# Attention's two score products per head: one wait for both banks, and the two issued side by side

## The chip, the cores and the metric

The kernel runs on one core of a Trainium2 chip. The metric is the device time of one execution in microseconds (us); lower is better. Of the kernel before there are three timed runs and one profiled execution.

## What is computed

The reference is a two-layer trunk over 512 tokens of width 1024. Each layer adds half a SwiGLU block, then a token mixer of four branches, then another half SwiGLU block:

```
for l in range(DEPTH):
    h = h + 0.5 * swiglu_ffn(rmsnorm(h, ...), ...)
    h = h + hybrid_token_mixer(rmsnorm(h, ...), l, ...)
    h = h + 0.5 * swiglu_ffn(rmsnorm(h, ...), ...)
return rmsnorm(h, final_norm)
```

The change is in the first branch, differential attention, with 4 heads. Each head has two sets of queries and keys (c = 0 and 1) of 64 channels each, and one set of values of 128 channels. A query sees the keys of its own chunk of 64 tokens and of all earlier ones:

```
s = jnp.einsum('bqhcd,bkhcd->bhcqk', q_blk, k)
p = jax.nn.softmax(jnp.where(allowed, s, -jnp.inf), axis=-1)
a = p[:, :, 0] - lam * p[:, :, 1]
return jnp.einsum('bhqk,bkhd->bqhd', a, v)
```

So each head and each block of 128 queries needs two score products that contract over only 64 channels. Everything is float32.

## The kernel before

The weights are streamed from HBM in tiles of 128x1024. Each tile is split into a rounded part `whi` (a CAST on ScalarE, L151) and a remainder `wlo` (a subtraction on VectorE), and every dense product runs as three one-pass products on TensorE. In the mixer's feature products these are the lines L157, L158 and L159. Eight k-steps of them, 24 products of 512 columns, make one output tile.

In each layer's mixer three things are issued in one stretch. The RWKV branch (`rwkv`) is one stream; attention (`diff_attn`), then GLA, then SSD are the other; and a `filler` of gate projections (`gate`: 24 products of L157 to L159, then a sigmoid on ScalarE into the tile `sg`, then a store by the SyncE queue) is put between their steps by `cotrace`, from costs written into the code. That fixes the order in which the code is traced. The order that each engine finally executes is then fixed when the program is built: a scheduler takes instructions by priority and by when it believes them ready. Each engine works through its own list in order and waits on semaphores. `chained(last, fn)` makes `fn`'s instruction stand behind `last` in that list; `prio(d)` shifts the priority.

Attention runs over 4 query blocks (qb 0 to 3) and in each over 4 heads (h 0 to 3). For a block the keys number n = 128, 256, 384 or 512. One head does this:

- two score products (L972), into two PSUM banks `sc[0]` and `sc[1]` of the tag `oy`, which has exactly two. The product of c = 0 reads partitions 0 to 63 of the queries and keys, that of c = 1 partitions 64 to 127. Since the operands are plain float32, each product is two instructions on TensorE. There are 16 heads and blocks a layer, so 64 products and 128 instructions in all;
- per bank a small memset for the mask (L974), a row maximum on VectorE (L976, `mx`), and an exponential with row sum on ScalarE (a helper, L100, tile `dap`), which shows as an ACTIVATE and an ACTIVATION_READ_ACCUMULATOR;
- on VectorE the scaling and the difference of the two, then transposes on TensorE (L987), a copy back on ScalarE (L989) and the products with the values (L993, `dv`).

The next head's products write the same two banks, so the product of c = 0 waits until the exponential of c = 0 of the head before has read its bank, and likewise for c = 1. Nothing ties the two products to each other.

Two more lines are named below. L761 is the last row of a triangular inversion that RWKV does row by row on VectorE in the same stretch; its result goes through two rounds of DMA to the products of L790. L647 and L634 are small TensorE steps of RWKV.

Of the kernel before, what the change touches and what calls it, by code (L numbers as in the profile page):

```python
# [13 lines left out]
AF = mybir.ActivationFunctionType  # L14
# [59 lines left out]
class Body:  # L74
# [815 lines left out]
    def diff_attn(self, ydst):  # L890
        nc = self.nc
        mm = nc.tensor.matmul
        dp = self.cp
        lam_init = 0.8 - 0.6 * math.exp(-0.3 * self.l)
        lam = self.g2((128, 256), name="lam")
        nc.sync.dma_start(out=lam, in_=self.a["lam"][self.l].partition_broadcast(128))
        lt = self.g2((128, 2, 64), name="lt")
        for j in range(2):
            self.mul(lt[:, j, :], lam[:, 128 * j : 128 * j + 64], lam[:, 128 * j + 64 : 128 * j + 128])
        ls = dp.tile([128, 2], F32, name="ls")  # L900
        nc.vector.tensor_reduce(out=ls, in_=lt, axis=AX.X, op=ALU.add)
        self.act(ls, ls, AF.Exp)
        nlam = dp.tile([128, 1], F32, name="nlam")
        self.sub(nlam, ls[:, 1:2], ls[:, 0:1])
        self.ts(nlam, nlam, -lam_init, ALU.add)
        gda = dp.tile([128, 1], F32, name="gda")
        self.ts(gda, self.p("da_n"), 1.0 - lam_init, ALU.mult)
        cos = self.c("cos").rearrange("p (t f) -> p t f", t=NT)
        sin = self.c("sin").rearrange("p (t f) -> p t f", t=NT)
        qT = []  # L910
        yield 0, 0

        def rope(ps, t, sc, sink):
            b = self.g2((128, 8, 2, 32), name="ropeb")
            o = self.g2((128, 16, 32), name="ropeo")
            c16 = cos[:, t : t + 1, :].to_broadcast([128, 16, 32])
            s8 = sin[:, t : t + 1, :].to_broadcast([128, 8, 32])
            p4 = ps.rearrange("p (h s f) -> p h s f", h=8, s=2)
            self.stt(o, ps.rearrange("p (h f) -> p h f", h=16), sc, c16, ALU.mult, ALU.mult)
            self.stt(b[:, :, 0, :], p4[:, :, 1, :], -sc, s8, ALU.mult, ALU.mult)  # L920
            self.stt(b[:, :, 1, :], p4[:, :, 0, :], sc, s8, ALU.mult, ALU.mult)
            of = o.rearrange("p h f -> p (h f)")
            self.add(of, of, b.rearrange("p h s f -> p (h s f)"))
            pt = self.small("os", (128, 4, 128))
            for h in range(4):
                nc.tensor.transpose(pt[:, h, :], of[:, h * 128 : (h + 1) * 128], self.ident)
            if isinstance(sink, list):
                for h in range(4):
                    nc.scalar.copy(sink[h][:, t * 128 : (t + 1) * 128], pt[:, h, :])
            else:  # L930
                nc.scalar.copy(sink, pt)

        def freed(pst):

            for t in range(2):
                o = self.g2(name="tk")
                nc.scalar.copy(o, pst[t])
                pst[t] = o
            return pst

        xs = (lambda k: self.xh[:, k, :], lambda k: self.xl[:, k, :])
        pk = self.tok(self.wt("dk"), *xs)
        kT = [self.g2(name="kT") for _ in range(4)]
        yield 20.8, 0.378
        pk = freed(pk)
        for t in range(NT):
            rope(pk[t], t, 1.0, kT)
            yield 0.4, 0.735
        pq = self.tok(self.wt("dq"), *xs)
        yield 20.8, 0.16  # L950
        pq = freed(pq)
        for t in range(NT):
            q = self.g2((128, 4, 128), name="qT")
            rope(pq[t], t, 0.125, q)
            qT.append(q)
            yield 0.4, 3
        pv = self.tok(self.wt("dv"), *xs)
        v = []
        for t in range(NT):
            vt = self.g2(name="dv")  # L960
            nc.scalar.copy(vt, pv[t])
            v.append(vt)
        yield 20.8, 0.702
        for qb in range(NT):
            n = (qb + 1) * 128
            o = self.g2((128, 4, 128), name="dao")
            for h in range(4):
                pr, l2 = [], dp.tile([128, 2], F32, tag="l2", bufs=2, name="l2")
                sc = [self.small("oy") for _ in range(2)]
                for c in range(2):  # L970
                    cp_ = slice(64 * c, 64 * c + 64)
                    mm(out=sc[c][:, 0:n], lhsT=qT[qb][cp_, h, :], rhs=kT[h][cp_, 0:n], start=True, stop=True)  # L972
                for c, s in enumerate(sc):
                    nc.vector.memset(s[0:64, n - 64 : n], -3.0e38)  # L974
                    mx = dp.tile([128, 1], F32, tag="mx", bufs=4, name="mx")
                    nc.vector.tensor_reduce(out=mx, in_=s[:, 0:n], axis=AX.X, op=ALU.max, negate=True)  # L976
                    e = self.g2(name="dap")
                    self.act(e[:, 0:n], s[:, 0:n], AF.Exp, bias=mx[:, 0:1], accum_out=l2[:, c : c + 1])
                    pr.append(e)
                r2 = dp.tile([128, 2], F32, tag="r2", bufs=2, name="r2")  # L980
                nc.vector.reciprocal(r2, l2)
                self.mul(r2[:, 1:2], r2[:, 1:2], nlam)
                self.ts(pr[0][:, 0:n], pr[0][:, 0:n], r2[:, 0:1], ALU.mult)
                self.stt(pr[0][:, 0:n], pr[1][:, 0:n], r2[:, 1:2], pr[0][:, 0:n], ALU.mult, ALU.add)
                pt = self.small("os", (128, 4, 128))
                for kb in range(qb + 1):
                    nc.tensor.transpose(pt[:, kb, :], pr[0][:, kb * 128 : (kb + 1) * 128], self.ident)  # L987
                at = pr[1].rearrange("p (k q) -> p k q", k=4)
                nc.scalar.copy(at[:, 0 : qb + 1, :], pt[:, 0 : qb + 1, :])  # L989
                po = self.small("os", (128, 128))  # L990
                last = None
                for kb in range(qb + 1):
                    last = self.chained(last, lambda: mm(  # L993
                        out=po, lhsT=at[:, kb, :], rhs=v[kb][:, h * 128 : (h + 1) * 128], start=kb == 0, stop=kb == qb))
                nc.vector.tensor_copy(o[:, h, :], po)
                yield 0.6 + 0.4 * qb, 2 + 0.7 * qb
            sq = self.g2((128, 4, 128), name="dasq")
            self.act(sq, o, AF.Square)
            ss = dp.tile([128, 4], F32, tag="das", bufs=2, name="das")
            nc.vector.tensor_reduce(out=ss, in_=sq, axis=AX.X, op=ALU.add)  # L1000
            self.ts(ss, ss, 1.0 / 128, ALU.mult, EPS, ALU.add)
            rs = dp.tile([128, 4], F32, tag="dar", bufs=2, name="dar")
            self.rsqrt(rs, ss, dp, "da")
            self.mul(o, o, rs.unsqueeze(2).to_broadcast([128, 4, 128]))
            pt = self.small("os", (128, 4, 128))
            for h in range(4):
                nc.tensor.transpose(pt[:, h, :], o[:, h, :], self.ident)
            self.act(o, pt, AF.Identity, scale=gda[:, 0:1])
            nc.sync.dma_start(out=ydst[:, :, qb * 128 : (qb + 1) * 128], in_=o)
            yield 0.4, 1.65  # L1010
# [465 lines left out]
```

## Time and profile before

| | |
|---|---|
| timed runs | 3089.2, 3090.36 and 3090.7 us; median 3090.36 |
| the profiled execution's own time | 3089.28 us, of which the profile's span is 3087.5 us |
| granted TensorE clock over the span | 0.998 of full speed |
| busy share of the span | TensorE 99%, VectorE 51%, ScalarE 37%, GpSimd 4% |
| stretches with attention's score products | 497 to 655 us (layer 0), 2031 to 2189 us (layer 1) |

An engine's share is an average over the whole program. What a change in one stage is worth is read in that stage: from the times at which instructions start there, and from what each waits for.

### The profile page before, as it was taken

What the parts mean: (1) busy time and instruction counts of PE and PEld (TensorE: products, weight loads), DVE (VectorE), ACT (ScalarE), POOL (GpSimd) and SP (SyncE); (2) the same over time, 40 slices, a digit from 0 to 9 for tenths busy, and PEclk for the clock granted to TensorE, in tenths of its full rate; (3) what the DMA queues carried; (4) which work ended last, traced back from release to release, by engine and by line L of the source; (5) the groups of instructions that cost most, each with busy time, mean ns of one, the idle gap of its engine ahead of it and who ended that gap; (6) DMA issues with size and microseconds to landing.
All of it is one profiled execution on the core that took longest, in us unless ns stands there. A gap on an engine that the chain in (4) does not pass through costs nothing. (4 is left out here: it accounts for less than half of the span.)

```text
span 3087.5 us, 40904 instructions
## 1 busy us (share of the span) xinstructions
PE 3044.8 (99%) x16212; PEld 2421.4 (78%) x16212; DVE 1587.4 (51%) x3229; ACT 1151.8 (37%) x1806; POOL 112.0 (4%) x148
## 2 busy tenths in 40 slices
PE   9999999999999999999999999999999999999999
PEld 7888887767777788888888888876777767888887
DVE  4332355857386875332343324558664968643323
ACT  4222345655332324222232223456544333232222
POOL 0000000001011100000000000000000111000000
PEclk9999999999999999999999999999999999999999
DMA  4222332322222554222342223223232325532222
GB/s 165 97 100 96 110 121 77 109 77 96 97 91 76 180 172 150 96 99 99 106 140 96 97 100 129 92 91 106 72 100 92 96 70 197 174 137 98 100 96 82
DMA packets 138450, 337.98 MB, mean 109 GB/s; under 512 B 35089, under 2 KB 43665, under 8 KB 137490
## 3 DMA queue, kind: packets, MB, share of 16 engines
q1 hardware_dynamic: 138112, 335.10, 32.7%
q8 instruction: 127, 2.08, 0.3%
q14 instruction: 65, 0.53, 0.1%
q10 hardware_dynamic: 146, 0.27, 0.0%
HBM read 297.03 MB, written 38.27 MB: 109 GB/s over the span
## 5 line engine op out<-in xcount | busy, mean ns | idle before, releaser
L81 DVE TENSOR_TENSOR wlo<-wraw,whi 128x1024 fp32r<-128x1024 f32 x478 | 585.3, 1225 | 873.2 <-ACT whi L151 859.7
L151 ACT CAST whi<-wraw 128x1024 fp32r<-128x1024 f32 x478 | 502.2, 1051 | 1397.6 <-PE pb L158 558.2
L157 PE MATMUL pb<-xh,whi 128*128 128x512 f32 x2064 | 821.2, 398 | 0.8 <-ACT s L100 0.8
L158 PE MATMUL pb<-xl,whi 128*128 128x512 f32 x2064 | 813.4, 394 | 0.0
L159 PE MATMUL pb<-xh,wlo 128*128 128x512 f32 x2064 | 809.8, 392 | 0.0
L157 PEld LDWEIGHTS pb<-xh,whi 128*128 128x128 f32 x2064 | 387.6, 188 | 98.5 <-issue 14.8
L158 PEld LDWEIGHTS pb<-xl,whi 128*128 128x128 f32 x2064 | 387.7, 188 | 81.9 <-issue 5.2
L159 PEld LDWEIGHTS pb<-xh,wlo 128*128 128x128 f32 x2064 | 387.8, 188 | 79.6 <-issue 1.0
L81 DVE TENSOR_TENSOR s<-s,pb 128x512 f32<-128x512 f32 x88 | 60.5, 687 | 303.0 <-PE pb L159 284.2
L100 ACT ACT_TABLE_LOAD x113 | 145.0, 1283 | 7.6 <-PE os L1252 3.9
L157 PE MATMUL pb<-yh,whi 128*128 128x512 f32 (+2 forms) x272 | 105.6, 390 | 0.0
L158 PE MATMUL pb<-yl,whi 128*128 128x512 f32 (+2 forms) x272 | 103.8, 382 | 0.7 <-DVE yl L81 0.7
L159 PE MATMUL pb<-yh,wlo 128*128 128x512 f32 (+2 forms) x272 | 103.6, 381 | 0.0
L157 PE MATMUL oy<-xh,whi 128*128 128x512 f32 x192 | 77.3, 403 | 5.8 <-DVE conv L97 5.5
L207 PE MATMUL pb<-whi,xh 128*128 128x512 f32 x192 | 76.6, 399 | 0.0
L158 PE MATMUL oy<-xl,whi 128*128 128x512 f32 x192 | 76.5, 398 | 0.0
L159 PE MATMUL oy<-xh,wlo 128*128 128x512 f32 x192 | 76.4, 398 | 0.0
L208 PE MATMUL oy<-wlo,xh 128*128 128x512 f32 x192 | 76.2, 397 | 0.0
L209 PE MATMUL pb<-whi,xl 128*128 128x512 f32 x192 | 76.1, 398 | 0.0
L207 PE MATMUL oy<-whi,xh 128*128 128x512 f32 x192 | 75.5, 393 | 0.0
L209 PE MATMUL oy<-whi,xl 128*128 128x512 f32 x192 | 75.5, 393 | 0.0
L208 PE MATMUL pb<-wlo,xh 128*128 128x512 f32 x192 | 75.5, 393 | 0.0
(421 smaller groups left out, 4570.8 us busy)
## 6 DMA issues: line engine op xcount, KB each, us to landing
wraw<-in_ffn_gu SPq DMA_DIRECT2D x176, 512.0 KB, 3.2
wraw<-in_win_f SPq DMA_DIRECT2D x118, 512.0 KB, 3.3
wraw<-in_ffn_d SPq DMA_DIRECT2D x88, 512.0 KB, 3.2
wraw<-in_win_t SPq DMA_DIRECT2D x48, 512.0 KB, 3.3
gd<-sg SPq DMA_DIRECT2D x64, 256.0 KB, 2.2
wraw<-in_wbr SPq DMA_DIRECT2D x32, 512.0 KB, 3.6
msg<-gd SPq DMA_DIRECT2D x64, 256.0 KB, 3.1
wraw<-in_wout SPq DMA_DIRECT2D x16, 512.0 KB, 3.2
```

The lines of the kernel that those rows point to most:

```text
L81: return (eng or self.nc.vector).tensor_tensor(out=out, in0=in0, in1=in1, op=op)
L100: return self.nc.scalar.activation(out=out, in_=in_, func=func, **kw)
L151: self.chained(behind[0], lambda: nc.scalar.copy(hi, raw))
L157: mm(out=ps, lhsT=lh, rhs=rh, start=first, stop=False)
L158: mm(out=ps, lhsT=lh, rhs=rl, start=False, stop=False)
L159: return mm(out=ps, lhsT=ll, rhs=rh, start=False, stop=last)
L207: mm(out=pst[t], lhsT=lh(k)[:, lt], rhs=hi[:, c], start=k == 0, stop=False)
L208: mm(out=pst[t], lhsT=lh(k)[:, lt], rhs=low[:, c], start=False, stop=False)
L209: mm(out=pst[t], lhsT=ll(k)[:, lt], rhs=hi[:, c], start=False, stop=k == nk - 1)
```

## The change

Three things are added, all in the loop over heads:

- ahead of a head's score products ScalarE copies one element into the first of the two banks. This copy is chained behind `ex`, the last exponential of the head before. As it writes the bank into which the product of c = 0 will go, that product has to wait for it;
- the product of c = 1 is chained behind that of c = 0, and its priority is moved up by 2000;
- the exponentials are chained to each other, through all heads and blocks.

```
+        ex = None
         for qb in range(NT):
             n = (qb + 1) * 128
             o = self.g2((128, 4, 128), name="dao")
             for h in range(4):
                 pr, l2 = [], dp.tile([128, 2], F32, tag="l2", bufs=2, name="l2")
                 sc = [self.small("oy") for _ in range(2)]
+
+                self.chained(ex, lambda: nc.scalar.copy(sc[0][0:1, 0:1], self.ident[0:1, 0:1]))
+                last = None
                 for c in range(2):
                     cp_ = slice(64 * c, 64 * c + 64)
-                    mm(out=sc[c][:, 0:n], lhsT=qT[qb][cp_, h, :], rhs=kT[h][cp_, 0:n], start=True, stop=True)
+                    with self.prio(-2000 * c):
+                        last = self.chained(last, lambda: mm(
+                            out=sc[c][:, 0:n], lhsT=qT[qb][cp_, h, :], rhs=kT[h][cp_, 0:n], start=True, stop=True))
                 for c, s in enumerate(sc):
                     nc.vector.memset(s[0:64, n - 64 : n], -3.0e38)
                     mx = dp.tile([128, 1], F32, tag="mx", bufs=4, name="mx")
                     nc.vector.tensor_reduce(out=mx, in_=s[:, 0:n], axis=AX.X, op=ALU.max, negate=True)
                     e = self.g2(name="dap")
-                    self.act(e[:, 0:n], s[:, 0:n], AF.Exp, bias=mx[:, 0:1], accum_out=l2[:, c : c + 1])
+                    ex = self.chained(ex, lambda: self.act(
+                        e[:, 0:n], s[:, 0:n], AF.Exp, bias=mx[:, 0:1], accum_out=l2[:, c : c + 1]))
                     pr.append(e)
```

Below the edit the line numbers of the changed kernel are 7 higher than before in most places: its score products are L977, its one-element copy L972, the transposes of the heads L994, the products with the values L1000.

The built order of the two kernels differs only in the stretch of attention in each layer: in layer 0 the lists of TensorE part at the second head of block 0 and agree again some 200 rows behind the score products of the last head of block 3, and layer 1 has the same differences. Before, the two products of a head stand next to each other in TensorE's list in 9 of the 16 heads of a layer; after the change in all 16. They stand apart before in h1 of block 0 (n = 128), h1 of block 1 (256), h0 and h2 of block 2 (384), and h1, h2 and h3 of block 3 (512). ScalarE's list gets 32 one-element copies, and its table loads go from 113 to 117.

On TensorE, at the second head of block 3 (n = 512), the two products before; `dap` is the head's probabilities, L796 and L790 are RWKV:

```order
L987 MATMUL os<-ident,dap 128x128
L159 MATMUL pb<-xh,wlo 128x512
L972 MATMUL oy<-kT,qT 128x512
L796 MATMUL rs<-tt,qt 32x32 [waits DMAHW5_49,Activation_49]
L796 MATMUL rs<-tt,qt 32x32 x14
L790 MATMUL rs<-xt_4471,am 32x32 [waits DMAHW6_49,PE_49]
L993 MATMUL os<-dv,dap 128x128 [waits Activation_49]
L993 MATMUL os<-dv,dap 128x128 x3
L972 MATMUL oy<-kT,qT 128x512
```

and after the change:

```order
L994 MATMUL os<-ident,dap 128x128 [waits DVE_49]
L994 MATMUL os<-ident,dap 128x128 x3
L159 MATMUL pb<-xh,wlo 128x512
L977 MATMUL oy<-kT,qT 128x512 [waits Activation_49]
L977 MATMUL oy<-kT,qT 128x512
L1000 MATMUL os<-dv,dap 128x128 [waits Activation_49]
L1000 MATMUL os<-dv,dap 128x128 x3
```

The two products have become neighbours, with one wait for ScalarE at the first; the RWKV products now come later.

On ScalarE, between the copies back of h0 and h1 of block 1 (n = 256), before; `sg` is a gate's sigmoid, and the exponentials of h1 are the rows with l_3990:

```order
L989 COPY dap<-os 128x256 [waits DVE_49,PE_49,Activation_49]
L151 CAST whi<-wraw 128x1024 [waits DMAHW6_49,PE_49]
L100 ACTIVATE dap,l_3990<-oy,mx 128x256
L100 ACTIVATE dap,l_3990<-oy,mx 128x256 [waits DVE_49]
L100 ACT_TABLE_LOAD [waits DMAHW7_49]
L100 ACTIVATE sg<-pb,prm 128x512 [waits PE_49]
L100 ACT_TABLE_LOAD
```

and after the change, where the exponentials of h1 are the rows with l_3995:

```order
L996 COPY dap<-os 128x256 [waits DVE_49,PE_49,Activation_49]
L151 CAST whi<-wraw 128x1024 [waits DMAHW6_49,PE_49]
L100 ACT_TABLE_LOAD [waits DMAHW7_49]
L100 ACTIVATE sg<-pb,prm 128x512 [waits PE_49]
L100 ACT_TABLE_LOAD [waits DVE_49]
L100 ACTIVATE dap,l_3995<-oy,mx 128x256 [waits Activation_49]
L100 ACTIVATE dap,l_3995<-oy,mx 128x256 [waits DVE_49]
L972 COPY oy<-ident 1x1 [waits Activation_49]
```

The gate's sigmoid, with a table load on either side, has moved ahead of the exponentials, and the one-element copy stands right behind them. All 32 copies wait, if at all, only for ScalarE's own earlier work.

On VectorE the inversion's last row L761 stands 12 rows ahead of the first memset of block 3's h0 before; after the change it stands two rows ahead of the first memset of h1, behind the scaling of h0's probabilities. On TensorE the first product of L790 stood ahead of h1's products and now stands behind them, with 23 one-pass products between.

## Rows read from the trace of the kernel before

**Rows 1.** The page, part 1: busy us, share of the span, instructions.
```profile
PE 3044.8 (99%) x16212; PEld 2421.4 (78%) x16212; DVE 1587.4 (51%) x3229; ACT 1151.8 (37%) x1806; POOL 112.0 (4%) x148
```

**Rows 2.** Windows: length, each engine's busy us, clock, DMA, in both attention stretches.
```profile
497.00:661.00 164.00, 161.44 (x1057) 112.84 (x1056) 116.62 (x366) 102.57 (x190) 7.93 (x16) 1.00 0.29 89
2031.00:2195.00 164.00, 161.84 (x1063) 113.18 (x1062) 116.58 (x366) 102.51 (x190) 7.93 (x16) 1.00 0.28 89
```

**Rows 3.** Source line L972: its TensorE instructions, duration in ns min/median/max, forms.
```profile
L972 PE MATMUL oy<-kT,qT x128: 272/482/694, 497.1 to 2188.5; 64*128 64x128 f32 x32, 64*128 64x256 f32 x32, 64*128 64x384 f32 x32, 64*128 64x512 f32 x32
```

**Rows 4.** Timeline, TensorE, 512 keys: start us, us, instruction, xcount.
```profile
611.39 1.13 PE L972 MATMUL oy<-kT,qT 64*128 64x512 f32 x4
612.45 0.50 PE L157 MATMUL pb<-xh,whi 128*128 128x512 f32 x1
612.78 0.39 PE L158 MATMUL pb<-xl,whi 128*128 128x512 f32 x1
613.01 0.40 PE L159 MATMUL pb<-xh,wlo 128*128 128x512 f32 x1
...
621.72 1.12 PE L972 MATMUL oy<-kT,qT 64*128 64x512 f32 x2
622.77 0.59 PE L796 MATMUL rs<-tt,qt 32*32 32x32 f32 x25
```

**Rows 5.** Timeline, TensorE, score products of 128, 256 and 384 keys.
```profile
508.86 0.48 PE L972 MATMUL oy<-kT,qT 64*128 64x128 f32 x2
...
516.90 0.49 PE L972 MATMUL oy<-kT,qT 64*128 64x128 f32 x4
...
531.91 0.70 PE L972 MATMUL oy<-kT,qT 64*128 64x256 f32 x4
...
536.81 0.70 PE L972 MATMUL oy<-kT,qT 64*128 64x256 f32 x2
...
544.27 0.97 PE L972 MATMUL oy<-kT,qT 64*128 64x256 f32 x4
...
581.88 0.92 PE L972 MATMUL oy<-kT,qT 64*128 64x384 f32 x4
...
588.39 0.91 PE L972 MATMUL oy<-kT,qT 64*128 64x384 f32 x2
```

**Rows 6.** Groups by form, ScalarE: busy us, mean ns, idle before.
```profile
L100 ACT ACT_TABLE_LOAD x113 | 145.0, 1283 | 7.6 <-PE os L1252 3.9 <-issue 1.8
...
L100 ACT ACTIVATION_READ_ACCUMULATOR dap<-oy,mx 128x1 f32 x64 | 12.6, 197 | 0.0
...
L100 ACT ACTIVATE nr<-ss,nms 128x1 f32<-128x1 f32 x28 | 8.3, 296 | 1.3 <-DVE hm L94 0.5
```

**Rows 7.** Timeline, ScalarE, block 1, h1.
```profile
542.52 1.05 ACT L151 CAST whi<-wraw 128x1024 fp32r<-128x1024 f32 x1 [1.03 <-PE pb L158]
543.47 0.46 ACT L100 ACTIVATE dap<-oy,mx 128x256 f32<-128x256 f32 x1
...
544.29 0.20 ACT L100 ACTIVATION_READ_ACCUMULATOR dap<-oy,mx 128x1 f32 x1
544.50 1.28 ACT L100 ACT_TABLE_LOAD   x1
545.80 0.69 ACT L100 ACTIVATE sg<-pb,prm 128x512 f32<-128x512 f32 x1
```

**Rows 8.** Timeline, TensorE, the two longest waits in layer 0's attention stretch.
```profile
527.57 0.30 PE L987 MATMUL os<-ident,dap 128*128 128x128 f32 x1 [0.60 <-DVE dap L97]
...
616.90 0.63 PE L1007 MATMUL os<-ident,dao 128*128 128x128 f32 x4 [0.96 <-DVE dao L81]
```

**Rows 9.** Timeline, TensorE, two small groups in block 1.
```profile
541.57 0.68 PE L993 MATMUL os<-dv,dap 128*128 128x128 f32 x4
...
547.35 0.60 PE L647 MATMUL rs<-ident,q 128*128 128x128 f32 x4
```

**Rows 10.** Timeline, VectorE and TensorE: the inversion's end and the first product behind it.
```profile
609.59 1.11 DVE L761 COPY nx<-xi 32x1024 f32<-32x1024 f32 x1
...
618.61 0.24 PE L790 MATMUL rs<-xt,am 32*32 32x32 f32 x2
```

More of the change, by code (lines that the diff above doesn't have):

```diff
@@ L963, in diff_attn @@
         yield 20.8, 0.702
+        ex = None
         for qb in range(NT):
@@ L969, in diff_attn @@
                 sc = [self.small("oy") for _ in range(2)]
+                self.chained(ex, lambda: nc.scalar.copy(sc[0][0:1, 0:1], self.ident[0:1, 0:1]))
+                last = None
                 for c in range(2):
                     cp_ = slice(64 * c, 64 * c + 64)
-                    mm(out=sc[c][:, 0:n], lhsT=qT[qb][cp_, h, :], rhs=kT[h][cp_, 0:n], start=True, stop=True)
+                    with self.prio(-2000 * c):
+                        last = self.chained(last, lambda: mm(
+                            out=sc[c][:, 0:n], lhsT=qT[qb][cp_, h, :], rhs=kT[h][cp_, 0:n], start=True, stop=True))
                 for c, s in enumerate(sc):
@@ L977, in diff_attn @@
                     e = self.g2(name="dap")
-                    self.act(e[:, 0:n], s[:, 0:n], AF.Exp, bias=mx[:, 0:1], accum_out=l2[:, c : c + 1])
+                    ex = self.chained(ex, lambda: self.act(
+                        e[:, 0:n], s[:, 0:n], AF.Exp, bias=mx[:, 0:1], accum_out=l2[:, c : c + 1]))
                     pr.append(e)
```

## The prediction, written before the changed kernel ran

> **What bounds the kernel now.** I began with the page's first part: TensorE is busy 3044.8 of 3087.5 us, every other engine at most half [rows 1]. So a microsecond is won or lost here only if TensorE works less or waits less. The windows over the two attention stretches, 164 us each, say the same of the place of the change: TensorE is busy for 161.44 and 161.84 us, idle for 2.6 and 2.2, at full clock; VectorE has some 117 and ScalarE some 103 busy microseconds there [rows 2]. Both helpers have a third of the stretch free, but not at every moment, and it is moments that count: TensorE takes its list in order.
>
> Then the source line of the score products: 128 instructions, that is 64 products of two instructions each, eight products for each width n and layer [rows 3]. Its medians say little, since an instruction lasts as long whether it runs alone or beside another. The timeline tells the two apart. At 512 keys four instructions that stand together, a head's two products, take 1.13 us from 611.39; two instructions, one product alone, take 1.12 us from 621.72 [rows 4]. Two products that start together cost the time of one: they use different halves of the contraction rows, and write different banks. The next instruction starts 1.06 us after the pair and 1.05 after the single one, so 0.07 us of either is a tail that overlaps what follows. It is the same at other widths: 0.49 against 0.48 us at 128, 0.70 against 0.70 at 256, 0.92 against 0.91 at 384 [rows 5].
>
> **What the change saves.** A product that stands alone costs its time without the tail; after the change the head costs one such time. By the built order seven heads a layer are apart now:
>
> - h1 of block 0 (128): 2 x (0.48 - 0.07) - (0.49 - 0.07) = 0.40 us;
> - h1 of block 1 (256): 2 x 0.63 - 0.63 = 0.63;
> - h0 and h2 of block 2 (384): 2 x 0.84 - 0.85 = 0.83 each, 1.66;
> - h1, h2, h3 of block 3 (512): 2 x 1.05 - 1.06 = 1.04 each, 3.12.
>
> One more head, h2 of block 1, has its products as neighbours, but they take 0.97 us where a pair takes 0.70 [rows 5]: the second waits for its own bank. With one wait for both that 0.27 goes too. Sum: 0.40 + 0.63 + 1.66 + 3.12 + 0.27 = 6.1 us a layer, and as layer 1 has the same order, 12.2 us in all. The other eight heads are pairs already and save nothing. This part rests on the list alone: each pair stands together in it, and what the second waited for, the first has waited for.
>
> **What it adds.** 32 one-element copies on ScalarE. The trace has none; the nearest rows are the row sum's read-out (197 ns) and a one-column ACTIVATE (296 ns) [rows 6]. The copy has no table and no sum, so nothing in it excludes less than either; it is between the two in what it does, and I take 0.25 us, 4 us a layer. ScalarE has 61 us free there [rows 2], and as the copies wait for ScalarE alone they hold nobody up behind them. The ScalarE Activation LUTs page of the Trainium skill (What ACT_TABLE_LOAD costs) puts an ACTIVATE with immediate scale and bias at 186 ns plus 0.833 ns an element; a copy at that price would be 6 us of ScalarE instead of 8, and the sum would stay. No run here shows it yet.
>
> Four more table loads of 1.283 us [rows 6], 2.6 us of ScalarE a layer, hidden by the same free time where they don't stand ahead of an exponential that TensorE needs.
>
> Chaining the exponentials costs nothing that I can see: they stood in that order already at the heads whose rows I read [rows 7].
>
> **What it moves: the waits.** The leading product may now start only after the last exponential and a copy. In block 1 that matters: the first product of h2 started at 544.27 [rows 5], while the last exponential of h1 ended at 544.49 [rows 7]. After the change, the list of ScalarE there is: the cast of a weight tile, released by the L158 right behind the pair of h1; a table load; the gate's sigmoid; a table load; the two exponentials; the copy. From the rows: the releasing product 0.39 [rows 4], then 1.05 + 1.28 + 0.69 + 1.28, the two exponentials 1.02 (543.47 to 544.49) [rows 7], the copy 0.25: 5.96 us. TensorE has between that product and the pair of h2 21 one-pass products at 0.23 us [rows 4], the values' products and L647, 0.68 and 0.60 with their tails [rows 9]: 6.1 us, or 5.7 without tails. So a wait between 0 and 0.3 us; I charge 0.2.
>
> Behind the waiting pair stand one-pass products and the heads' own later work, which would be late by as much and no more.
>
> The rest of the order has shifted by a few rows too, and a wait can come or go at any of them. The bounds: the longest waits now are 0.60 and 0.96 us, both for VectorE [rows 8], and all idle time of the stretch is 2.6 us [rows 2]. In block 3 the inversion's steps stand between those of h0's softmax after the change, so that the transposes of h0 may wait about as long as the longest now. I take half of that, 0.5 us, which lies nearer to no change than to a second 0.96, as VectorE has 47 us free. Below nothing: 1 us of today's waits might go as well. Above: twice today's idle time, 2.6 us a layer. With the 0.2 it is 0.7 us a layer, 1.4 in all.
>
> **Sum.** 12.2 - 1.4 = 10.8 us off the profiled execution's own 3089.28 us: 3078.5. That execution lies 1.1 us under the median of the timed runs, 3090.36, so I forecast 3079 us against this median, 0.35% less.
>
> **Rivals.**
>
> *The softmax behind the pair becomes the bound.* Two banks filled at once are not two banks emptied at once: two maxima, two exponentials and now a copy stand between a pair and the next. For it: a table load, a sigmoid and a second load, 3.25 us [rows 7], now stand ahead of exponentials that ran right behind the cast before, and there are two loads more a layer. Against it: 117 and 103 of 164 us [rows 2], and the list leaves about 6 us at the tightest place. If one such 3.25 us a layer lies open, 6.5 us come back: 12.2 - 1.4 - 6.5 = 4.3, some 3086 us. The Trainium skill has this as a rule (TensorEngine Tiling (Array Packing), Performance Considerations): tiling speeds up TensorE, not the emptying of PSUM, and the copy out may become the bottleneck. By that rule the sum is 3086, by the rows 3079; that both emptying engines are free for a third of the stretch speaks against the rule here.
>
> *Slower: RWKV's inversion comes late.* VectorE ends it at 610.70 now, and the first L790 behind its DMAs starts at 618.61, 7.9 us later [rows 10]. After the change the end has moved behind the scaling of block 3's h0, and between that scaling and L790 TensorE has a pair (1.06), 23 one-pass products (5.3), the values' products (some 1.1, twice as many as 0.68 with its tail) and two sets of four transposes (0.60 a set with its tail) [rows 4, 9], together about 8.4 us. L761 itself (1.11) and three short steps come off that: some 6.9 us. If the DMAs need all of 7.9, TensorE waits 1 us a layer, and the time is 3081. Slower than before by 0.2% it would be only if the wait were 9 us a layer (12.2 + 6.2, over two), that is, if the whole inversion were pushed back. Then some 3097 us or more. VectorE's free third speaks against it.
>
> *It doesn't do what it says.* The pair stands together in the list, but the second product starts late all the same, or the first waits where both would have been free: then the time stays at 3090. Against it: the four such pairs whose rows I read ran in the time of one product [rows 4, 5], and what the second waited for stands now ahead of the first.
>
> **Chances.** Forecast 0.75, the softmax 0.15, no effect 0.05, slower 0.05. 0.2% of the time is 6.2 us, about what a measurement of this kernel can tell from no change. Faster by more than that, below 3084.2: the forecast and a third of the softmax's case, 0.80. Within: the rest of it and no effect, 0.15. Slower: 0.05. The forecast's own range is 3076 (a microsecond of today's waits goes in each layer: 12.2 + 2 = 14.2 less) to 3083 (waits of 2.6 us a layer: 7.0 less). For 8 in 10 I go on to 3074.5 below, as the widths' prices may be off by a tenth, and to 3086 above, the softmax's case.
>
> **What would show it.** Right: in the changed kernel's timeline every pair starts within some 10 ns and appears as four instructions of 0.49, 0.70, 0.92 and 1.13 us; TensorE's busy time falls by about 12 us, idle time in the stretch stays below 4 us a layer; the copies last 0.2 to 0.3 us. Wrong: score products that wait for ScalarE, above all in block 1; L790 waiting for a DMA; long idle time at the transposes of block 3's h0; or differences outside the two stretches, where the lists are the same and nothing should move.

## The result, and the profile after

| | before | after |
|---|---|---|
| median of the timed runs | 3089.78 us (4 runs, 3089.16 to 3090.7) | 3073.09 us (4 runs, 3072.59 to 3073.43) |
| profiled execution, its span | 3087.5 us | 3071.6 us |

The ratio is 0.9946 with a 95% interval of 0.9934 to 0.9959: the change takes 16.7 us away. The forecast was 3079 us, 10.8 us less than before, and its range ended at 3074.5. The sign and the main mechanism were right; the gain is half as large again as was worked out, so the time lies below the range.

The page of the changed kernel, part 1 (busy us, share of the span, instructions), answers to [rows 1]:

```profile
PE 3029.6 (99%) x16212; PEld 2415.4 (79%) x16212; DVE 1579.9 (51%) x3229; ACT 1158.4 (38%) x1842; POOL 116.4 (4%) x148
```

TensorE's busy time falls by 15.2 us for the same 16212 instructions. ScalarE has 36 instructions more, the 32 copies and four table loads. The windows over the two attention stretches (columns as in [rows 2]; 162 us each, as the stretches are shorter now):

```profile
496.00:658.00 162.00, 159.84 (x1082) 114.91 (x1080) 115.06 (x364) 109.09 (x212) 9.83 (x16) 1.00 0.31 95
2020.00:2182.00 162.00, 159.83 (x1063) 114.92 (x1061) 114.32 (x362) 110.35 (x214) 9.38 (x15) 1.00 0.31 95
```

TensorE is idle for 2.2 us in each, about as long as before, at the same full clock. So the time came out of TensorE's own work and not out of its waits. The source line of the copies, and TensorE's timeline at pairs of 128, 256, 384 and 512 keys (as [rows 4, 5]):

```profile
L972 ACT COPY oy<-ident x32: 143/144/152, 496.1 to 2156.8; 1x1 f32<-1x1 f32 x32
```

```profile
508.27 0.49 PE L977 MATMUL oy<-kT,qT 64*128 64x128 f32 x4
...
530.98 0.70 PE L977 MATMUL oy<-kT,qT 64*128 64x256 f32 x4
...
593.92 0.92 PE L977 MATMUL oy<-kT,qT 64*128 64x384 f32 x4
...
607.53 0.39 PE L159 MATMUL pb<-xh,wlo 128*128 128x512 f32 x1
607.85 1.13 PE L977 MATMUL oy<-kT,qT 64*128 64x512 f32 x4
608.91 0.50 PE L157 MATMUL pb<-xh,whi 128*128 128x512 f32 x1
609.24 0.39 PE L158 MATMUL pb<-xl,whi 128*128 128x512 f32 x1
```

Each head but the first of a layer shows as one row of four instructions, in the time of a single product. In the trace the second product starts 6 to 7 ns behind the first in all heads but that one, h0 of block 0, whose pair was interleaved with L698 already before. The last three rows hold something that the sum had passed over: a one-pass product starts 0.23 us behind the one ahead of it, but the pair starts 0.32 us behind its row, and the row behind the pair has 0.33 us to the next.

Block 1, where the forecast saw a wait, on ScalarE (as [rows 7]) and at the same place on TensorE:

```profile
544.92 0.47 ACT L100 ACTIVATE dap<-oy,mx 128x256 f32<-128x256 f32 x1
545.27 0.20 ACT L100 ACTIVATION_READ_ACCUMULATOR dap<-oy,mx 128x1 f32 x1
545.37 0.14 ACT L972 COPY oy<-ident 1x1 f32<-1x1 f32 x1
```

```profile
545.34 0.40 PE L158 MATMUL pb<-xl,whi 128*128 128x512 f32 x1
545.66 0.70 PE L977 MATMUL oy<-kT,qT 64*128 64x256 f32 x4
```

The copy is over at 545.51 and the pair of h2 starts at 545.66, 0.32 us behind its row. Twelve pairs of the layer stand behind a one-pass product: nine start 0.32 to 0.33 us behind it, and three, whose row itself stands right behind other work, 0.40 us. So this pair doesn't wait, with 0.15 us to spare. (The profile puts 0.35 us of idle time of the weight loads down to the copy here, but they are idle for as long ahead of most other pairs.) The waits of TensorE over 0.15 us in layer 0's stretch, in us in total, times, and the longest; the stretch of layer 1 prints the same:

```profile
PE os L994 <- DVE dap L97: 1.1, 2, 0.7
PE os L1014 <- DVE dao L81: 0.4, 1, 0.4
PE rs L720 <- DVE am L81: 0.2, 1, 0.2
```

All are for VectorE, none for ScalarE's copy and none at L790. The wait of 0.96 us at L1007, the transposes of block 2's finished output [rows 8], is gone; the longest is now 0.67.

**Where 15.9 us of the span went.** I compared the two traces over each layer's stretch, from the first score product to the 520th one-pass product behind it, by the time from each instruction's start to the next one's, with idle time apart. Per layer (layer 0, layer 1): the score products 18.22 to 12.05 us, -6.17 in both; the other instructions -1.90 and -1.91; idle time -0.40 and 0.00. Together that is 16.55 us. Ahead of the first stretch the changed kernel is 0.59 us ahead, and behind the second it loses 1.4 us again. Both lie within what the traces of all the kernels here differ by at these places: the first score product starts at 496.2 to 497.8 us, and 849.8 to 852.5 us follow the second stretch.

### The profile page after: what moved, and what is told of

Read it like the earlier page. It is cut to its first block, busy times and chain, and to the rows that moved or that the text cites. A ratio compares the mean times of both kernels' runs of the same rounds, so it can differ in the third digit from the quotient of the medians.

```text
span 3071.6 us, 40997 instructions
## 1 busy us (share of the span) xinstructions
PE 3029.6 (99%) x16212; PEld 2415.4 (79%) x16212; DVE 1579.9 (51%) x3229; ACT 1158.4 (38%) x1842; POOL 116.4 (4%) x148
```

## The experiments

Each timed ratio is against the kernel before, run on the same chip. The first four ran beside a before of 3089.37 us, the next four beside 3089.80, the last two beside 3089.02. "Changed kernel" is the one of the result.

### One part alone: the pair without the copy

```
-                self.chained(ex, lambda: nc.scalar.copy(sc[0][0:1, 0:1], self.ident[0:1, 0:1]))
...
-                    ex = self.chained(ex, lambda: self.act(
-                        e[:, 0:n], s[:, 0:n], AF.Exp, bias=mx[:, 0:1], accum_out=l2[:, c : c + 1]))
+                    self.act(e[:, 0:n], s[:, 0:n], AF.Exp, bias=mx[:, 0:1], accum_out=l2[:, c : c + 1])
```

> The chaining of the second product behind the first and its priority alone: no one-element copy, no chain of the exponentials. In the built order 15 of 16 heads a layer have neighbours (h1 of block 1 has not). Theory A, TensorE's work (two products in the time of one, 6.2 us a layer in the changed kernel's trace, and about 1.9 us from cheaper neighbours of other instructions): 2 x (6.2 - 0.6) from the pairs and 1 to 2 from neighbours, 12 to 13.5 us less than before, some 3077 us. Theory B, the gain comes from the one wait for both banks (fewer or shorter waits): at most 5 us, 3085 or more, and second products that start late.

Measured: 3078.35 us, ratio 0.9963 (0.9949 to 0.9977). That is 11 us less than before, far from theory B's 5 at most, and 1 us short of theory A's 12 to 13.5. In the trace the score products lose 5.17 us a layer, the other instructions 1.07, and idle time grows by 0.70 and 1.14 us. TensorE's timeline at h1 and h2 of block 1:

```profile
536.66 0.70 PE L976 MATMUL oy<-kT,qT 64*128 64x256 f32 x2
...
537.95 0.70 PE L976 MATMUL oy<-kT,qT 64*128 64x256 f32 x2
...
544.13 0.96 PE L976 MATMUL oy<-kT,qT 64*128 64x256 f32 x4
```

The chain and the priority alone bring most of the pairs together. What the copy and the chain of the exponentials add (no run parts these two) is the last of them (h1 of block 1 is apart here), the common wait (h2 still takes 0.96 us instead of 0.70), and another order around the heads: the changed kernel is 5 us faster.

### The other part alone: the copy without the pair

```
-                    with self.prio(-2000 * c):
-                        last = self.chained(last, lambda: mm(
-                            out=sc[c][:, 0:n], lhsT=qT[qb][cp_, h, :], rhs=kT[h][cp_, 0:n], start=True, stop=True))
+                    mm(out=sc[c][:, 0:n], lhsT=qT[qb][cp_, h, :], rhs=kT[h][cp_, 0:n], start=True, stop=True)
```

> The one-element copy and the chained exponentials, without chaining the two products. In the built order 11 of 16 heads a layer have neighbours, 2 more than before (h1 of block 1, h1 of block 3). Theory A: those two heads are worth 0.6 + 1.0, the lagging one 0.3, 1.9 us a layer, 3.9 in all; with neighbours priced from the traces up to 7; 3083 to 3086 us. Theory B: nearly the whole 16 us, 3073 to 3076.

Measured: 3079.5 us, ratio 0.9966 (0.9953 to 0.9979). The score products lose 2.0 us a layer, where 1.9 was expected, but the time falls by two and a half times what this gives: the other instructions lose 2.6 us a layer, and idle time 0.71 and 0.31. So neither number of the two theories held, and 2.6 us a layer came from instructions that the change doesn't touch. In the changed kernel that part is 1.9 us. It is a term that the sum had left out.

### Two products that stand together but can't run together

```
+                        if c:
+                            last = self.chained(last, lambda: mm(
+                                out=sc[1][:, 0:2], lhsT=self.c("bones"), rhs=self.c("hsel"), start=True, stop=True))
```

This puts a product of 128 rows and two columns between the two score products. The next kernel puts the same one ahead of the pair (`if not c`, and unchained).

> The changed kernel with a small product of two columns over all 128 rows put between a head's two score products, so that they can't run together; its result is overwritten. Theory A: each head costs two product times again, in all 16 heads a layer, 11.6 us a layer more than in the changed kernel, and the small products and the two switches of shape 3 to 4 us a layer: about 3100 to 3106 us, 10 to 16 over the kernel before. Rival C, the gain is in the order of the rest and in the waits, not in the two products running together: 3073 and 2 to 3.5 us a layer for the small products, 3077 to 3080.

> The same small product, but ahead of the pair, which stays together: the control of the one before. Theory A: the changed kernel and 2 to 3.5 us a layer, 3077 to 3081 us; its distance to the kernel with the small product between is 23 us (two layers of 16 heads whose second product costs its time again). Rival C: no distance between the two beyond 2 us.

Measured: 3100.91 us, ratio 1.0037 (1.0025 to 1.0048), with the product between, and 3076.52 us, ratio 0.9958 (0.9943 to 0.9973), with the product ahead: 24.4 us apart where 23 were expected; the score products' own time is 11.1 us a layer longer, 22 of the 24.4. TensorE's timeline of the first at a head of 128 keys:

```profile
516.94 0.48 PE L980 MATMUL oy<-kT,qT 64*128 64x128 f32 x2
517.36 0.38 PE L978 MATMUL oy<-cst 128*128 128x2 f32 x2
517.67 0.49 PE L980 MATMUL oy<-kT,qT 64*128 64x128 f32 x2
518.08 0.50 PE L157 MATMUL pb<-xh,whi 128*128 128x512 f32 x1
```

The two score products pay 0.42 and 0.41 us one after the other instead of 0.42 once. What the change wins with the pairs is that two products run at the same time; that they stand near each other, or wait once, is not enough.

### The pair right behind the transposes of the head before

```
-        ex = None
+        ex = tp = None
...
-                last = None
+                last = tp
...
-                    with self.prio(-2000 * c):
+                    with self.prio(-2000):
...
-                    nc.tensor.transpose(pt[:, kb, :], pr[0][:, kb * 128 : (kb + 1) * 128], self.ident)
+                    tp = nc.tensor.transpose(pt[:, kb, :], pr[0][:, kb * 128 : (kb + 1) * 128], self.ident)
```

> Copy, chains and pairs as in the changed kernel, but the leading product is also chained right behind the last transpose of the head before, so that in 14 of 16 heads a layer transposes and pair stand together, with no three-row group between them. Theory A (TensorE's own time: the pairs, and what an instruction costs beside its neighbour): the pairs stay together and keep their gain; in the changed kernel a head takes 28 ns from its last transpose to the row after it and 318 ns from a row to a pair, here 202 ns from transpose to pair and 227 ns from a row to the next row, 83 ns more, times 28 heads: 2.3 us slower than the changed kernel, 3074.5 to 3077 us, with the whole loss in what stands ahead of the pairs and in the rows there. Rival B (what was won over the forecast is waits that went): the price beside a neighbour counts for nothing, and the time is that of the changed kernel, 3073, or goes with the sum of idle time in the attention stretches, whichever way that turns.

Measured: 3075.98 us, ratio 0.9953 (0.9938 to 0.9967), beside 3072.66 us for the changed kernel on the same chip. The number is in theory A's range, and yet its reason falls. Rival B falls too: idle time in the stretch is 0.6 us a layer less than in the changed kernel, and the time is longer. TensorE's timeline, first of the changed kernel (transposes alone; a pair alone stands above at 607.85), then of this one (both together):

```profile
649.51 0.39 PE L158 MATMUL pb<-xl,whi 128*128 128x512 f32 x1
649.74 0.60 PE L994 MATMUL os<-ident,dap 128*128 128x128 f32 x4
650.09 0.47 PE L159 MATMUL pb<-xh,wlo 128*128 128x512 f32 x1
650.41 0.39 PE L157 MATMUL pb<-xh,whi 128*128 128x512 f32 x1
```

```profile
618.52 0.40 PE L157 MATMUL pb<-xh,whi 128*128 128x512 f32 x1
618.76 0.60 PE L994 MATMUL os<-ident,dap 128*128 128x128 f32 x4
619.29 1.13 PE L977 MATMUL oy<-kT,qT 64*128 64x512 f32 x4
620.35 0.50 PE L158 MATMUL pb<-xl,whi 128*128 128x512 f32 x1
620.68 0.40 PE L159 MATMUL pb<-xh,wlo 128*128 128x512 f32 x1
```

From the start of the row ahead to the start of the second row behind, less two rows at 0.228: transposes alone 0.44 us, the pair alone 1.71 - 0.46 = 1.25, together 2.16 - 0.46 = 1.70. What the transposes lose beside the pair is what the rows between would have lost. So a price can't be read off one instruction and its neighbour, as I had done for this expectation; it has to be taken over a whole group with the rows at both its ends. The loss of this kernel has another place: the products of L600 and L601, which use different halves and ran at the same time in the changed kernel, are parted here by the values' products (timelines of the changed kernel and of this one):

```profile
522.89 0.59 PE L601 MATMUL rs<-rwa,lor 64*128 64x512 f32 x1
522.89 0.59 PE L600 MATMUL rs<-rwa,lor 64*128 64x512 f32 x1
```

```profile
524.74 1.02 PE L600 MATMUL rs<-rwa,lor 64*128 64x512 f32 x2
525.96 0.49 PE L1000 MATMUL os<-dv,dap 128*128 128x128 f32 x2 [0.20 <-ACT dap L996]
526.38 1.12 PE L601 MATMUL rs<-rwa,lor 64*128 64x512 f32 x2
```

These four instructions take 1.1 us more a layer, of 1.4 us that TensorE works more in the stretch than in the changed kernel. With the idle time that went, the two stretches are 1.7 us longer; the rest of the 3.3 us lies outside them, where its cause stays open (between the stretches the changed kernel's own two traces differ by 1.5 us).

### The copy on VectorE

```
-                self.chained(ex, lambda: nc.scalar.copy(sc[0][0:1, 0:1], self.ident[0:1, 0:1]))
+                self.chained(ex, lambda: nc.vector.tensor_copy(sc[0][0:1, 0:1], self.ident[0:1, 0:1]))
```

> As the changed kernel, with the one-element copy on VectorE in place of ScalarE (it still comes behind the last exponential, whose sums it doesn't need but whose bank it waits for). Theory A: 30 of the 32 pairs stay together (one a layer is parted, 0.4 to 0.6 us each), the rest as in the changed kernel: 3073 to 3075.5 us. Rival D (ScalarE's copy costs something there, behind the exponentials and ahead of the transposes' copies): without it ScalarE's queue moves on some 0.15 us earlier in each head, 32 times, and the kernel ends up to 4.8 us sooner than the changed one, 3068 to 3072.

Measured: 3083.65 us, ratio 0.9981 (0.9971 to 0.999): 11 us slower than the changed kernel, which neither theory expected. The source line of the copy and what VectorE waited for ahead of it (us, times):

```profile
L972 DVE COPY oy<-ident x32: 135/142/152, 496.8 to 2166.4; 1x1 f32<-1x1 f32 x32
...
  ACT dap L100: 12.3, 8
  ACT dv L961: 6.0, 2
```

The copy is as short there (135 to 152 ns). But VectorE takes its list in order too, and at ten of the 32 copies it stands still for ScalarE, 18.3 us in all. Behind the copy stand the steps for which TensorE waits: its idle time is 5.8 us in each stretch instead of 2.3, and the score products, with one pair a layer apart, keep 5.2 of 6.17 us. On ScalarE the copy waits for nobody, as the exponential that it follows is on the same engine.

### The same idea at another place

```
-                for c in range(NC):
-                    cs = slice(c * 64, c * 64 + 64)
-                    mm(out=pa[vp, c, :], lhsT=u[hp, cs], rhs=e[hp, cs], start=True, stop=True)
+            for c in range(NC):
+                cs = slice(c * 64, c * 64 + 64)
+                for h in range(2):
+                    hp, vp = slice(64 * h, 64 * h + 64), slice(64 - 64 * h, 128 - 64 * h)
+                    mm(out=pa[vp, c, :], lhsT=u[hp, cs], rhs=e[hp, cs], start=True, stop=True)
```

> As the changed kernel, and in the gated linear attention the 64-row products of the two halves (128 instructions in four groups of 32) are issued alternately, one of each half, where now all 16 instructions of one half stand ahead of those of the other. There is no wait between them on either side, so it shows whether the halves alone make the gain. Theory A: where one half follows itself an instruction starts 58 ns behind the last; where halves alternate, 5 and 54 ns by turns (seen at the one place where they meet in each group). Half of some 120 starts go from 58 to 5: about 3.2 us less, 3069 to 3071, with those groups at about 0.95 us each where they took 1.8. Rival C (only what waits on a bank wins by standing together; these run on nothing else): 3073, the groups as long as before.

> The changed kernel once more, so that the three others have it beside them on the same chip: 3072 to 3074.5 us by every theory.

Measured: 3069.09 us (3068.54 to 3069.23), ratio 0.993 (0.9916 to 0.9945), against 3072.66 us for the changed kernel, ratio 0.9943 (0.9928 to 0.9958). One of the four groups on TensorE's timeline, in the changed kernel and in this one:

```profile
710.88 1.90 PE L1098 MATMUL os<-e,u 64*64 64x64 f32 x32
712.70 0.50 PE L157 MATMUL pb<-xh,whi 128*128 128x512 f32 x1
```

```profile
711.54 1.15 PE L1100 MATMUL os<-e,u 64*64 64x64 f32 x32
712.62 0.50 PE L157 MATMUL pb<-xh,whi 128*128 128x512 f32 x1
```

From the group's start to the next row it is 1.08 us instead of 1.82, 0.74 less, four times: 3.0 of the 3.6 us measured, where 3.2 were expected. TensorE waits for nothing here, at the groups' first products or behind them, so the two halves alone make the gain. This kernel is faster than the kernel before and than the changed one.

### What a group of its own costs

A product of 64 rows and two columns for each head is added to the changed kernel: first ahead of the pair, on the half of the rows that the leading product uses; then free to go as soon as its bank is, on the other half and into the other bank.

```
+                        if not c:
+                            last = mm(out=sc[0][:, 0:2], lhsT=self.c("bones")[0:64], rhs=self.c("hsel")[0:64], start=True, stop=True)
```

```
+                    if not c:
+                        with self.prio(-4000):
+                            mm(out=sc[1][:, 0:2], lhsT=self.c("bones")[64:128], rhs=self.c("hsel")[64:128], start=True, stop=True)
```

> As the changed kernel, with a 64-row product of two columns directly ahead of each pair, on the half of the rows that the leading product uses (32 more products of two instructions; the pair's leading product overwrites what it writes). Theory E (a group of 64-row work has a price at its edges, where it meets one-pass rows: the row ahead of it takes 0.32 instead of 0.23 us, the row behind it 0.33, 0.19 together, which the sum of the prediction left out): the small product stands inside the edges that the pair pays anyway, so it costs its own time alone, some 0.1 us (two instructions at about 52 ns), 1.7 us a layer: about 3076 us. Rival F (edges have no price, or each product brings its own): the same as in the kernel where the small products stand apart, whichever that is.

> The same small product, now not chained to the pair and allowed to go as early as its bank is free: in the built order 11 of 16 a layer have one-pass rows on both sides, and two more stand with one side on rows. Theory E: 11 new groups a layer with two edges each, 0.19 us beside the product's own 0.1: 1.7 + 2.1 = 3.8 us a layer more than the changed kernel, about 3080.5 us, 4 us behind the kernel with the small products ahead of the pairs; in the timeline the rows beside them take 0.32 and 0.33 us. Rival F: no difference beyond 1 us between the two kernels.

Measured: 3078.0 us, ratio 0.9963 (0.995 to 0.9976), and 3088.43 us, ratio 0.9998 (0.9989 to 1.0008). They are 10.4 us apart, where 4 were expected. TensorE's timeline of the second at one small product among one-pass rows, then of the first at a pair of 256 keys:

```profile
518.45 0.39 PE L159 MATMUL pb<-xh,wlo 128*128 128x512 f32 x1
518.77 0.38 PE L978 MATMUL oy<-cst 64*128 64x2 f32 x2
519.08 0.50 PE L157 MATMUL pb<-xh,whi 128*128 128x512 f32 x1
519.41 0.40 PE L158 MATMUL pb<-xl,whi 128*128 128x512 f32 x1
```

```profile
532.34 0.39 PE L159 MATMUL pb<-xh,wlo 128*128 128x512 f32 x1
532.66 0.27 PE L978 MATMUL oy<-cst 64*128 64x2 f32 x1
...
533.50 0.50 PE L157 MATMUL pb<-xh,whi 128*128 128x512 f32 x1
533.84 0.39 PE L158 MATMUL pb<-xl,whi 128*128 128x512 f32 x1
```

In the first of these, from the row ahead to the second row behind it is 0.96 us; less two rows, the small product costs 0.50 us. Ahead of the pair of 256 keys it costs 0.21 (the whole group 1.50 - 0.46 = 1.04 us instead of 0.83). At the other places where two rows stand on either side and TensorE doesn't wait it is the same, 0.51 to 0.52 and 0.21 to 0.22. In the two stretches TensorE works 4.26 us a layer more with the products apart, and waits 0.8 us more; two layers of that are 10.2 of the 10.4 us. So theory E holds: 64-row work that is alone among one-pass products pays for its edges. The price was expected too low: beside 0.19 us on the two rows, the small product itself has 0.31 us to the next row, where all it adds in front of a pair is 0.21. So a group that is kept apart costs 0.3 us (0.50 - 0.21) beside its own time.

## Why the prediction was wrong in size

**What the change saves: right.** 6.1 us a layer was worked out for the seven heads that were apart and the one with two waits; the score products lost 6.17 in each layer. The kernel with the 128-row product put between the two shows that this is concurrency. (3090.36 less 10.8 is 3079.6; it was written as 3079.)

**What it adds: right that it is hidden, too dear in size.** A copy takes 0.144 us, below both bounds (0.197 and 0.296) and below the 0.25 that I took. The figure that the ScalarE Activation LUTs page of the Trainium skill gives for an ACTIVATE (What ACT_TABLE_LOAD costs), 186 ns, is nearer but too high as well. It moves nothing in the sum, except that at 0.25 us the pair of h2 in block 1, with 0.15 us to spare, would be nearly late.

**What it moves, the waits: the smaller step that failed.** 0.7 us a layer was charged, 0.2 at block 1's h2 and 0.5 at the transposes of block 3's h0. Neither wait came; idle time went by -0.40 and 0.00 us a layer. That is 1.8 of the 5.75 us that the stretches gave beyond the forecast. The second charge was half of a row of before, taken for a place that had no row; it lay within the bounds, which reached to 1 us a layer of gain.

**The term that is missing, the larger step that failed: the neighbours.** The sum counted a product from its start to the next start, and took everything else as unchanged, so that what the neighbours lose stood at nothing, without a reason. The other instructions lost 1.9 us a layer, 3.8 of the 5.75. The missing price can be seen in the kernel before, at h1 of block 1 (TensorE's timeline), one of the places that the prediction spoke of:

```profile
537.77 0.40 PE L159 MATMUL pb<-xh,wlo 128*128 128x512 f32 x1
538.10 0.70 PE L972 MATMUL oy<-kT,qT 64*128 64x256 f32 x2
538.72 0.50 PE L157 MATMUL pb<-xh,whi 128*128 128x512 f32 x1
539.06 0.40 PE L158 MATMUL pb<-xl,whi 128*128 128x512 f32 x1
539.29 0.39 PE L159 MATMUL pb<-xh,wlo 128*128 128x512 f32 x1
```

The second product of that head, at 538.10, costs 0.62 us by its start and the next one, but the row ahead of it takes 0.33 us and the row behind 0.34, where 0.23 is usual (539.06 to 539.29): 0.83 us in all (1.29 from 537.77 to 539.06, less two rows). I put 0.63 into the sum.

So where one-pass products stand on both sides, a product that is parted from its partner makes two places more at which an instruction over all 128 rows stands beside one over fewer. In TensorE's order there were 129 such places a layer before and are 111 after (at the score products themselves, 37 and 27). At 0.1 us, which is what the row ahead and the row behind each lose, 18 fewer come to 1.8 of the 1.9 us. The same estimate gives 1.2 us with the pair alone, where 1.07 were measured, 1.4 with the copy on VectorE (1.5 and 1.7), 0.8 with the pair behind the transposes (0.5, with the 1.1 us at L600 and L601 against it), but 1.6 with the copy alone, where it was 2.6. So it isn't a fixed price. Nor is it lost where the last two experiments measured it: the one-pass products hold only 0.2 of the 1.9 us, and the rest lies in small groups, 0.5 at the heads' transposes, 0.3 at the outputs' transposes (L1007) and 1.1 at RWKV's 64-row products (L735 to L852), while the products with the values cost 0.2 more. The last transpose of a head, for one, has 0.20 us to a product of fewer rows that follows, and at most places 0.03 to a one-pass product. That cheaper neighbours make up the 1.9 us is thus an estimate from these counts; no experiment shows it for the changed kernel itself, and the price of each kind of neighbour stays open.

**The rivals.** That the softmax behind the pair becomes the bound: the exponentials of block 1's h1 end 1 us later than before, but no pair waits for them, and none of TensorE's waits over 0.15 us there is for ScalarE. The rule of the Trainium skill that I weighed (TensorEngine Tiling (Array Packing), Performance Considerations) says that the copy out may become the bottleneck after a fourfold speedup. It doesn't bind here, where two products run at once, with VectorE busy for 115 and ScalarE for 109 of 162 us. The copy on VectorE shows how near it is all the same: a copy for which VectorE stands still brought 3.5 us a layer of waits. That the inversion comes late: no wait at L790. (The terms listed for it add up to 8.5 to 8.7 us, not 8.4, which speaks a little more against that rival.) That it doesn't do what it says: all pairs stand together, and all but h0 of block 0, which was so before, run so.

## What to carry to other kernels

Where two products use different halves of the contraction rows, put them next to each other in the list and make the first wait for whatever the second needs; look for loops that issue one half after the other, since turning such a loop round won 3.6 us here with two more lines. When such a product is priced among work of another shape, count from the row ahead to the second row behind and subtract the rows, since its edges lie in its neighbours. A wait that is put in by hand belongs on the engine that the awaited work runs on: in this kernel it held nobody up there, and on the other engine it cost 11 us.

## What the runs showed of the hardware that was not expected

- A group of 64-row work between one-pass products of 128 rows costs about 0.3 us beside what it costs next to other 64-row work: 0.09 us on the row ahead, 0.10 us on the row behind, and 0.1 us on itself. Four transposes of 128 rows at 649.51 have 0.23 us from the row ahead, as between rows (up to 0.40 at other places), but the row behind them has 0.32 us too.
- The second product of a pair starts 6 to 7 ns behind the first, and the two take the time of one; a 128-row product of two columns put between them takes this away (0.42 and 0.41 us one after the other).
- A one-element copy takes 0.144 us on ScalarE and 0.142 on VectorE.
